# A hybrid attention and DeltaNet layer: the values' convolution is issued behind the turns of queries and keys, one filling step per head is issued later, and the roots of the queries' scales behind the keys'

## The chip, the cores and the metric

The kernel runs on one core of a Trainium2 chip. The metric is the time of one execution on the device in microseconds; lower is better. The names of the engines are those of the profile: PE is the matrix engine, PEld its loading of weights, DVE, ACT and POOL the vector, scalar and general engines, SP the engine that issues nearly all DMAs here, one after another from its own queue.

## The reference

One layer over 1024 latent tokens and 256 context tokens, 1024 wide. What touches the change:

```python
h  = rmsnorm(x, g_pre) * (1.0 + scale[:, None]) + shift[:, None]
na_q, na_k, na_v, na_z, g_qkv, g_z, g_b, g_a = jnp.split(h @ w_in, IN_SPLITS, axis=-1)
...
o_na = neighborhood_attention(heads(na_q), heads(na_k), heads(na_v), heads(na_kc), heads(na_vc), rpb)
q, k, v = gdn_qkv(g_qkv, conv_w)          # convolution of 5 taps, silu, l2norm of q and k
q, k = axial_rope(q, rope), axial_rope(k, rope)
...
t_inv = lax.linalg.triangular_solve(eye + a, ...)     # a: strictly lower k k^T * decay, per 64 rows
...
state, o = lax.scan(step, state0, (u, w, qk, q_dec, k_dec, g_last))
...
y = jnp.concatenate([o_na * jax.nn.silu(na_z), o_g * jax.nn.silu(g_z)], axis=-1) @ w_out
x = x + gate[:, None] * rmsnorm(y, g_post)
```

There are 8 attention heads of 64 (four pairs) and 4 DeltaNet heads of 128, each run forward and backward. The context takes the same path and gives the scan its first state.

## The kernel before, in words

**Stages.** Everything is one program over five stages. `phase0` makes the modulated and normalised activations, each kept as a high and a low part (`hh`, `hl`), and the first projections. `phase2` (L806) takes the four DeltaNet heads in turn. `phase_a2` (L1452) does what is left of the projections and builds the inverses. `phase_b` (L1504) runs attention and the scan side by side. `phase4` multiplies by `w_out` and writes the output. The program is straight-line code; a scheduler in the framework, which follows a timeline of its own, decides the order of each engine's queue from the order in which the code is written, from buffers, and from a few forced edges (`order`, L151). So the queue of an engine isn't the order of the source.

**Projections.** Each product with `w_in` is three matmuls per slice of 128 input channels (`mm_chan`, L470; `mm_tok`, L482; both issue through the helper `mm`, so nearly all projection matmuls have the line L157): high by high, low weight by high, high by low. An output tile of 512 tokens costs 24 matmuls, a values tile (264 columns) also 24. `load_w` (L447) brings the weights, copies the high part on ACT and subtracts the low part on POOL (L464).

**A head of `phase2`.** For head h the function `step` is called with letters. Q, K and V are `conv` (L877): the projection of one 128-wide chunk (`gpl_q`, `gpl_k`, `gpl_v`, 48 matmuls of 512 tokens; keys and values also 24 of 256 context tokens), a copy by ACT, four taps on DVE and a tanh. T is `qk_tok` (L910): PE transposes the convolved queries and keys (`tp`), ACT squares them, POOL makes the keys' root (`rsqrt`, L174: an addition L176 and a power L177, named `rq_y_g`), and DVE and POOL scale and rotate them into `tok`; the queries' sums of squares are only collected in `ssq`. B is `qk_back` (L950): PE turns `tok` back (`tb`) into `kq`. U turns the convolved values (`vtp`). G, once, makes the gates. F is `delta_front` (L1024) of the head before: five pairs of tiles, each with matmuls of keys by keys and queries (`pk`, L1040 and L1042, in `phase2` with operand `kq`), DVE multiplications into `pm` and `qe`, and stores; at its end the lower triangles go to `ab_dram` (L1058). R is `res_gate` (L418): a small product with the adaLN weights (`parg`), its copy by ACT (`growg`), one more matmul (`pg`), two DVE operations and a store. A letter p takes one step of the generator `projections` (L865): six steps of gate projections for DeltaNet heads 1 to 3 (`pz`), seven for attention pair 1, five of two values tiles each (`pv`), fourteen for pairs 2 and 3 (`pq`, `pk`, `pz`; 32 steps in all). This is work for PE that waits for nothing of the heads, "filling" below.

The letters of a head are Q, K, then F of the head before, then `RVppTppUB`. For heads 2 and 3 the inverse blocks 0 and 1 (`inv_groups`, L1071) are woven in, a piece behind each letter: 31 pairs of DVE operations (L1090, L1093) that need the triangles of three heads' tiles, 120 rows a block. After head 3, F of head 3 follows.

**`phase_a2`.** Three filling steps are taken first, then the remaining ones, with pieces of inverse block 2 (80 rows, in `ab_vv`) and of the merges in between; what is left of both comes after. A merge (`inv_merge`, L1101) of a head combines the 32-row inverses to 128 rows by small matmuls (`tz`, `tu`), with copies between on DVE, ACT and POOL (L1149), and stores the result (`tm_dram`). Merges of heads 2 and 3 need inverse block 2, and so F of head 3.

**`phase_b`.** Each unit of attention is a set of matmuls `sc` (L763, L766), a softmax on DVE and ACT (`nm` L770, `pt` L771), a mask addition on POOL (`gm` L754) and matmuls by the values (`tc`, `tr`, `po`). All PE work of this stage is forced into the order of the code (`pe`, L606). The scan's matmuls stand between: `pa` L1272 (with `tm`), L1283 and L1254. Its operands are loaded by `delta_load` (L1189): `tm` 1280 KB, `v` and `kt` 640 KB each, `kq` 1152 KB, `qe` 1024 KB for a head. When h is 0 this function also calls `rsqrt` for the queries' scales (`rq_y_rho`, 128 x 32 values), which need only the four heads' `ssq` and are first used at the end of a scan.

## Time and profile before

| | before |
|---|---|
| median of 3 runs | 879.14 us (872.26, 879.24, 879.14) |
| profiled execution | 871.81 us |
| its span | 870.1 us |
| mean granted clock of TensorE | 0.97 |
| PE busy | 822.1 us (94%) |
| DVE, ACT, POOL busy | 503.3, 418.4, 355.7 us |
| DMA | 159.65 MB, mean 183 GB/s |

The profile is of one execution. Times in it count from the start of its span; `phase2` begins about 108 us, F of head 3 ends at 438, the first `sc` of `phase_b` starts at 551.07 and the output stage takes about the last 90 us. A timeline row gives start, duration, engine, source line, operation, output and inputs, and in brackets how long the engine was idle before and what ended that. A row that stands for several instructions has its count behind an x. Matmuls overlap, so what one costs is read from the distance between starts. PEclk is the granted clock of TensorE (1.00 is full speed).

### The profile page before, as it was taken

To read this page: it belongs to the slowest core of one execution; us is meant where nothing else is said; L and a number is where in the kernel's file an instruction comes from. 1 tells how busy PE (TensorE), PEld (TensorE's weight loads), DVE (VectorE), ACT (ScalarE), POOL (GpSimd) and SP (SyncE) were. 2 spreads that over 40 slices of the span, in tenths; PEclk is the share of its full clock that TensorE was granted. 3 is DMA by queue.
4 is the path that set the end of the run, shared out by engine and by line. 5 is a ranking of instruction groups with operands and counts; after the bars stand their busy time and mean duration, and the time that the engine had idled before them with its cause. 6 is when DMAs were issued, how large, how long until landed. Compare 5 with 4: busy or idle time off the path is not lost.

```text
span 870.1 us, 16462 instructions
## 1 busy us (share of the span) xinstructions
PE 822.1 (94%) x6082; PEld 698.2 (80%) x6082; DVE 503.3 (58%) x1051; ACT 418.4 (48%) x1087; POOL 355.7 (41%) x430
## 2 busy tenths in 40 slices
PE   6999999999999988988998998899999999999996
PEld 4788887888788776878886787788888988878885
DVE  3447165546635699869928953456666566653342
ACT  5356225744654653455315333466666666734210
POOL 2424031644362471228352100655657559624110
PEclk9999999999999998999999897699999999999998
DMA  9886442264454725652797489994967935134251
GB/s 334 315 286 224 133 134 88 83 202 160 123 187 150 210 85 164 201 136 67 239 257 236 155 202 309 415 226 127 303 177 260 252 96 180 41 110 133 86 185 68
DMA packets 86054, 159.65 MB, mean 183 GB/s; under 512 B 18373, under 2 KB 45334, under 8 KB 83798
## 3 DMA queue, kind: packets, MB, share of 16 engines
q1 hardware_dynamic: 78486, 144.94, 52.8%
q10 hardware_dynamic: 7488, 13.67, 5.1%
q8 instruction: 48, 0.79, 0.4%
q14 instruction: 32, 0.26, 0.1%
HBM read 109.51 MB, written 52.42 MB: 186 GB/s over the span
## 4 chain that ended last, share of the span: by engine, by line
PE 62%; DVE 16%; DMA 13%; ACT 3%; issue 3%; POOL 2%; SPq 1%; DVEq 0%; POOLq 0%; ACTq 0%
PE pz L157 5%; PE gpl_k L157 4%; PE gpl_q L157 4%; PE py L1381 3%; PE py L1382 3%; PE py L1383 3%; PE pk L157 3%; PE pv L157 3%; DVE vb L1093 3%; DVE tb L1090 3%; PE gpl_v L157 3%; PE pa L1272 3%; PE pq L157 2%; PE po L801 2%; PE pa L1283 2%
## 5 line engine op out<-in xcount | busy, mean ns | idle before, releaser
L771 ACT ACTIVATE pt<-pt,nm 128x544 f32<-128x544 f32 (+1 forms) x64 | 50.5, 790 | 38.2 <-DVE nm L770 37.9
L770 DVE CUSTOM_DVE_ANT_0 pt<-sc,gm 128x544 f32<-128x544 f32 (+1 forms) x64 | 49.4, 771 | 32.2 <-PE sc L766 26.5
L754 POOL TENSOR_TENSOR gm<-gt,mk 128x288 f32<-128x288 f32 (+1 forms) x48 | 46.6, 974 | 29.3 <-DVE nm L770 28.9
L1244 POOL TENSOR_SCALAR kd<-kt,kd 128x128 f32<-128x128 f32 x72 | 42.9, 609 | 21.2 <-PE pa L1283 21.1
L1032 ACT ACTIVATE em<-em,gc 128x128 f32<-128x128 f32 x80 | 25.6, 391 | 30.8 <-DMA em<-gc_dram 30.6
L157 PE MATMUL pz<-hh,wh_gz 128*128 128x512 f32 x96 | 38.2, 398 | 0.0
L157 PE MATMUL pv<-wh_nv,hh 128*128 128x264 f32 x128 | 36.7, 292 | 1.4 <-DVE st_z L568 0.8
L157 PE MATMUL pz<-hl,wh_gz 128*128 128x512 f32 x96 | 37.9, 395 | 0.0
L157 PE MATMUL pz<-hh,wl_gz 128*128 128x512 f32 x96 | 37.8, 393 | 0.0
L157 PE MATMUL pv<-wh_nv,hl 128*128 128x264 f32 x128 | 36.5, 288 | 1.1 <-DVE hl L273 1.1
L157 PE MATMUL pv<-wl_nv,hh 128*128 128x264 f32 x128 | 35.9, 286 | 1.4 <-DVE wl_nv L464 1.4
L1149 POOL COPY tm<-ld 32x320 f32<-32x320 f32 x16 | 7.3, 456 | 69.4 <-PE tz L1173 30.2
L899 DVE SCALAR_TENSOR_TENSOR acc_v<-xp_v,cols,acc_v 128x1282 f32<-128x1282 f32 x16 | 29.1, 1819 | 10.9 <-ACT acc_v L897 10.6
L1286 DVE SCALAR_TENSOR_TENSOR s<-s,egl,pa 128x128 f32<-128x128 f32 x64 | 19.6, 343 | 27.2 <-PE pa L1283 27.2
L1443 DVE TENSOR_TENSOR finv<-py,ggb 128x512 f32<-128x512 f32 x16 | 10.9, 689 | 41.7 <-ACT finv L1442 41.6
L1051 POOL TENSOR_SCALAR_AFFINE_SELECT qe<-qe 128x256 f32<-128x256 f32 x32 | 24.4, 765 | 25.0 <-DVE qe L1050 24.5
L1090 DVE TENSOR_TENSOR tb<-ab,vb 120x31 f32<-120x31 f32 (+15 forms) x62 | 29.1, 470 | 9.4 <-DMA ab<-ab_dram 7.8
L1250 POOL TENSOR_SCALAR vb<-v,beta 128x128 f32<-128x128 f32 x40 | 24.3, 608 | 20.9 <-DVE y L1256 17.8
L1442 ACT ACTIVATE finv<-py 128x512 f32<-128x512 f32 x16 | 9.5, 598 | 47.4 <-PE py L1383 29.3
L784 PE MATMUL tr<-c,pt 128*96 128x128 f32 (+1 forms) x192 | 32.0, 276 | 0.0
L782 ACT COPY tcx<-tc 128x256 f32<-128x256 f32 x64 | 23.5, 367 | 16.1 <-PE tc L780 15.7
L1047 DVE SCALAR_TENSOR_TENSOR pm<-pk,beta,em 128x128 f32<-128x128 f32 x80 | 23.6, 342 | 12.9 <-PE pk L1040 10.9
(432 smaller groups left out, 2857.6 us busy)
## 6 DMA issues: line engine op xcount, KB each, us to landing
wada<-in_w_ada SPq DMA_DIRECT2D x16, 512.0 KB
em<-gc_dram SPq DMA_DIRECT2D x20, 256.0 KB
pm_dram<-pm SPq DMA_DIRECT2D x20, 256.0 KB
tm_dram<-tm SPq DMA_DIRECT2D x8, 640.0 KB
kk<-qk_dram SPq DMA_DIRECT2D x16, 320.0 KB
tm<-tm_dram SPq DMA_DIRECT2D x4, 1280.0 KB
kq_dram<-kq SPq DMA_DIRECT2D x4, 1152.0 KB
kq<-kq_dram SPq DMA_DIRECT2D x4, 1152.0 KB
```

Source lines behind the costliest of these rows:

```text
L157: r = self.nc.tensor.matmul(*a, **k)
L754: r = nc.gpsimd.tensor_tensor(self.gm[hh][:, 384 - n:384].rearrange("p (n c r) -> p n c r", c=nco, r=4), gv, self.mk[:, mo:mo + n].rearran ...
L770: nc.vector.tensor_tensor_reduce(pt[:, 384 - n:], sc[:, 512 - n:768], gm[:, 384 - n:], -1.0, 3.0e38, ALU.add, ALU.min, nm)
L771: self.last_exp = nc.scalar.activation(pt[:, 384 - n:], pt[:, 384 - n:], AF.Exp, bias=nm, scale=-1.0, accum_out=sums[:, ct, hh:hh + 1]).in ...
L784: self.pe(nc.tensor.transpose(pl[:m, rc * P:(rc + 1) * P], pt[:, 384 + (rc - 3) * m:384 + (rc - 2) * m], self.ident))
L899: nc.vector.scalar_tensor_tensor(av, xp[:, s0 + tap:s0 + tap + 1282 - s0], wc(tap), av, ALU.mult, ALU.add)
L1090: nc.vector.tensor_tensor(t3, bc(ab[:, 0:m, m:m + 1], [r, m, n]), bc(vb[:, m:m + 1, m:], [r, m, n]), ALU.mult)
L1093: nc.vector.tensor_tensor(vb[:, 0:m, m:], vb[:, 0:m, m:], t3, ALU.subtract)
L1244: r = nc.gpsimd.tensor_scalar(kd[d], kt_[:, t, :], self.kd[:, h, d, t:t + 1], None, ALU.mult)
L1272: self.pe(nc.tensor.matmul(pa, tm[:, d, t, :], y[d], start=True, stop=True))
L1381: nc.tensor.matmul(py, mh[:, tt], wh[:, nn], start=(k == W_ORDER[0]), stop=False)
L1382: nc.tensor.matmul(py, ml[:, tt], wh[:, nn], start=False, stop=False)
```

## The change

Four edits, and no instruction is added to or removed from the computation.

1. The letters of a head become `RpTVrppBU`. The values' convolution V is written behind the turns T of queries and keys, B ahead of U, and three filling steps stand in a head instead of four.
2. `phase_a2` takes five filling steps ahead of its woven part instead of three. With 12 steps in `phase2` and 5 after it, 15 remain for the woven part; before, these were 16, 3 and 13.
3. `res_gate` becomes a generator in two parts. R does the loads, the `parg` matmuls and the ACT copy; the new letter r does the rest, and its `pg` matmul is ordered behind the projection matmul written last (`last_mm`).
4. `rsqrt` can be told to stand behind another instruction on POOL. The queries' roots are ordered behind the last root written before them, which is that of head 3's keys.

```diff
--- before.py
+++ after.py
@@ -155,6 +155,7 @@
 
     def mm(self, *a, **k):
         r = self.nc.tensor.matmul(*a, **k)
+        self.last_mm = r.ins.name
         if self.seq:
             self.pe(r)
 
@@ -171,10 +172,12 @@
             self.nc.sync.dma_start(self.dbg[name], ap)
 
 
-    def rsqrt(self, pool, x, n, tag, eps):
+    def rsqrt(self, pool, x, n, tag, eps, behind=None):
         y = pool.tile([P, n], F32, name=f"rq_y_{tag}", tag=f"rq_y{n}")
-        self.nc.gpsimd.tensor_scalar(y, x, eps, None, ALU.add)
-        self.nc.gpsimd.tensor_tensor(y, y, bc(self.mhalf, [P, n]), ALU.pow)
+        r = self.nc.gpsimd.tensor_scalar(y, x, eps, None, ALU.add)
+        if behind:
+            self.order(r, behind)
+        self.last_rsqrt = self.nc.gpsimd.tensor_tensor(y, y, bc(self.mhalf, [P, n]), ALU.pow).ins.name
         return y
 
 
@@ -432,16 +435,18 @@
             nc.tensor.matmul(par[g:g + 32, :], self.sc[:, k, :], w, start=(k < 4), stop=(k >= 4), tile_position=(0, g))
         rows = cv.tile([P, 256], F32, name=f"growg{q}", tag="grow", bufs=1)
         nc.scalar.copy(rows, par)
+        yield
         v = I["vecs"]
         br = st(f"br{q}")[:1, :].rearrange("p (a n) -> p a n", a=2)
         nc.sync.dma_start(br[:, 0, :], bass.AP(v.tensor, 40 * P + n, [[0, 1], [1, 256]]))
         nc.sync.dma_start(br[:, 1, :], bass.AP(v.tensor, 108 * P + n, [[0, 1], [1, 256]]))
         pg = ps.tile([P, 512], F32, name=f"pg{q}", tag="ta", bufs=3)
-        nc.tensor.matmul(pg[:1, :256], self.sel[:, 0:1], rows, start=True, stop=True)
+        self.order(nc.tensor.matmul(pg[:1, :256], self.sel[:, 0:1], rows, start=True, stop=True), self.last_mm)
         nc.vector.tensor_tensor(br[:, 0, :], pg[:1, :256], br[:, 0, :], ALU.add)
 
         nc.vector.scalar_tensor_tensor(br[:, 0, :], br[:, 0, :], float(D) ** 0.5, br[:, 1, :], ALU.mult, ALU.mult)
         nc.sync.dma_start(self.gg_dram[:, n:n + 256], br[:, 0, :])
+        yield
 
 
     def load_w(self, pool, c0, n, tag, bufs=(3, 4, 4), halves=2, load=None, ks=None, dst=None):
@@ -812,9 +817,10 @@
             nc.sync.dma_start(rope, I["rope"])
             self.ssq = self.cp.tile([P, 4, 8], F32, name="ssq")
             self.fill, self.ready = self.projections(cv), []
-            kq, conv, toks = {}, {}, {}
+            kq, conv, toks, gate_row = {}, {}, {}, None
 
             def step(h, c):
+                nonlocal gate_row
                 if c in "QKV":
                     i = "QKV".index(c)
                     conv[c] = self.conv(cv, ps, 4 * i + h, f"{'qkv'[i]}{h}", i > 0)
@@ -825,7 +831,10 @@
                 elif c == "F":
                     self.delta_front(cv, ps, h, kq[h])
                 elif c == "R":
-                    self.res_gate(cv, ps, h)
+                    gate_row = self.res_gate(cv, ps, h)
+                    next(gate_row)
+                elif c == "r":
+                    next(gate_row)
                 elif c == "T":
                     toks[h] = self.qk_tok(cv, ps, h, conv["Q"], conv["K"], rope)
                 elif c == "B":
@@ -853,7 +862,7 @@
                 step(h - 1, "F") if h else step(h, "G")
                 if h > 1:
                     blocks = self.inv_groups((h - 2,), lambda nm, n: cv.tile([P, n], F32, name=nm, tag=nm[:2]))
-                for c in "RVppTppUB":
+                for c in "RpTVrppBU":
                     step(h, c)
                     next(blocks, None)
             step(3, "F")
@@ -1199,7 +1208,8 @@
         self.scan_loads = self.last_load
         if h == 0:
 
-            self.rho = self.rsqrt(self.cp, self.ssq.rearrange("p h t -> p (h t)"), 32, "rho", 4 * EPS)
+            self.rho = self.rsqrt(self.cp, self.ssq.rearrange("p h t -> p (h t)"), 32, "rho", 4 * EPS,
+                                  self.last_rsqrt)
             self.rho2 = self.cp.tile([P, 32], F32, name="rho2")
             nc.gpsimd.tensor_tensor(self.rho2, self.rho, self.rho, ALU.mult)
         return kq, v, kt_, *(w.rearrange("p (d t) c -> p d t c", d=2) for w in (tm, qe))
@@ -1481,7 +1491,7 @@
             pr, gens = self.fill, (blocks(), merges())
             credit = [0.0, 0.0]
             first = True
-            for _ in range(3):
+            for _ in range(5):
                 next(pr)
             for _ in pr:
                 for i, (g, r) in enumerate(zip(gens, (3, 3))):
```

Three places show how the queues are changed. Rows are in the order of the queue; a count stands at the end of a row.

**PE at the end of head 3.** `tb` are turned keys and queries, `vtp` turned values, `pk` with operand `kq` the matmuls of F of head 3 (L1040 and L1042 before, L1049 and L1051 now), `pq` a filling projection of attention pair 2, `pv` a values tile. Before:

```order
L157 MATMUL pq_0_4306<-hh,wh_nq_4_4301 128x512
L157 MATMUL pq_0_4306<-hl,wh_nq_4_4301 128x512
L157 MATMUL pq_0_4306<-hh,wl_nq_4_4302 128x512
L1042 MATMUL pk_2_4074<-kq_4012 128x256 x2
L1042 MATMUL pk_4_4096<-kq_4012 128x256 x2
L157 MATMUL pq_0_4306<-hh,wh_nq_4_4301 128x512
L157 MATMUL pq_0_4306<-hl,wh_nq_4_4301 128x512
L157 MATMUL pq_0_4306<-hh,wl_nq_4_4302 128x512
L1042 MATMUL pk_6_4118<-kq_4012 128x256 x2
L157 MATMUL pq_1_4337<-hh,wl_nq_0_4296 128x512
```

Now:

```order
L965 MATMUL tb_1_6_3783<-c_60,tok_1_6_3476 128x128 x4
L847 MATMUL vtp_0_3796<-c_60,acc_v_3564 128x128 x2
L1051 MATMUL pk_2_3847<-kq_3757 128x256 x2
L1051 MATMUL pk_4_3869<-kq_3757 128x256 x2
L847 MATMUL vtp_2_3802<-c_60,acc_v_3564 128x128 x4
L1051 MATMUL pk_6_3891<-kq_3757 128x256 x2
L847 MATMUL vtp_6_3810<-c_60,acc_v_3564 128x128 x4
L1051 MATMUL pk_8_3913<-kq_3757 128x256 x2
L157 MATMUL pv_0_4068<-wh_nv_0_3987,hh 128x264
```

Before, the last of these `pk` (`pk_8`, 17 rows further down, behind 16 more `pq`) had all 240 values matmuls and 43 `pq` matmuls ahead of it. Now 48 values matmuls are ahead of it, the other 192 and all of `pq` of pair 2 come behind it, and the values of head 3 are turned between its pieces.

**SP from the end of `phase_a2` to `phase_b`.** `tm_dram<-tm` stores a merge, `qk_dram`, `z_dram` store projections, and `tm<-tm_dram`, `v`, `kt`, `kq`, `qe` are the loads of scan head 0. Before:

```order
L545 DMA qk_dram<-sl_k_5627 128x512
L569 DMA z_dram<-st_z_5669 128x512
L163 DMA kk_0_5373<-qk_dram 64x1280 x2
L569 DMA z_dram<-st_z_5698 128x512
L163 DMA kk_1_5382<-qk_dram 64x1280 x2
L1186 DMA tm_dram_87<-tm_4389 128x1280
L163 DMA tm_5742<-tm_dram_85 128x2560
L1186 DMA tm_dram_87<-tm_4391 128x1280
L163 DMA v_5740<-vt_dram_81 128x1280
L163 DMA kt_5741<-kt_dram_77 128x1280
L163 DMA kq_5739<-kq_dram_69 128x2304
L163 DMA qe_5743<-qe_dram_89 128x2048
```

Now:

```order
L1195 DMA tm_dram_88<-tm_4316 128x1280
L549 DMA qk_dram<-sh_k_5626 128x512
L550 DMA qk_dram<-sl_k_5627 128x512
L1195 DMA tm_dram_88<-tm_4317 128x1280
L164 DMA zs_0_5724<-z_dram 128x512
L164 DMA zs_1_5726<-z_dram 128x512
L574 DMA z_dram<-st_z_5669 128x512
L574 DMA z_dram<-st_z_5698 128x512
L164 DMA tm_5742<-tm_dram_85 128x2560
L164 DMA v_5740<-vt_dram_81 128x1280
L164 DMA kt_5741<-kt_dram_77 128x1280
L164 DMA kq_5739<-kq_dram_69 128x2304
L164 DMA qe_5743<-qe_dram_89 128x2048
```

The last two `z_dram` stores, of the last gate projection, stand directly ahead of the scan's loads. The buffers of these loads lie where the weights of the last projection were, so the first load also waits for PE's last projection matmul. On PE, 43 matmuls of that projection (19 of one tile, 24 of the next) now stand between the last `tu` of the last merge and the first `sc`; before, the last of them stood ahead of the closing products (L1173 to L1181) of the merges of heads 2 and 3.

**POOL at the roots.** `rq_y_rho` are the queries' roots, `rq_y_g` those of head 3's keys, `wl_nv` the low part of the values' weights. Before:

```order
L176 TENSOR_SCALAR rq_y_rho<-ssq 128x32
L945 TENSOR_TENSOR tok_1_6_3781<-tok_1_6_3781,rot_16_3795 128x512
L177 TENSOR_TENSOR rq_y_rho<-rq_y_rho,mhalf 128x32
L176 TENSOR_SCALAR rq_y_g_3836<-ss_3799 128x10
L1204 TENSOR_TENSOR rho_5752<-rq_y_rho 128x32
L177 TENSOR_TENSOR rq_y_g_3836<-rq_y_g_3836,mhalf 128x10
```

Now:

```order
L177 TENSOR_SCALAR rq_y_g_3531<-ss_3494 128x10
L180 TENSOR_TENSOR rq_y_g_3531<-rq_y_g_3531,mhalf 128x10
L177 TENSOR_SCALAR rq_y_rho<-ssq 128x32
L180 TENSOR_TENSOR rq_y_rho<-rq_y_rho,mhalf 128x32
L1214 TENSOR_TENSOR rho_5752<-rq_y_rho 128x32
L469 TENSOR_TENSOR wl_nv_4_4000<-wr_nv_4_3998,wh_nv_4_3999 128x528
```

The queries' roots came ahead of the keys' power, and now come behind it, ahead of a low part of the values' weights (`wl_nv_4`), which stood earlier in the queue before.

## The prediction

> **What bounds the kernel now.** I read the page's busy shares first, then the stages, then the waits of PE inside them, then the way from head 3 to the scan.
>
> ```profile
> PE 822.1 (94%) x6082; PEld 698.2 (80%) x6082; DVE 503.3 (58%) x1051; ACT 418.4 (48%) x1087; POOL 355.7 (41%) x430
> ```
>
> PE is busy nearly all the time, so only two things can shorten this kernel: time in which PE stands idle, and time in which its clock is halved. The view by stretches says where these are (length, busy time of PE, PEld, DVE, ACT, POOL with counts; then granted clock, DMA share, GB/s):
>
> ```profile
> 102.00:300.00 198.00, 198.00 (x1063) 164.91 (x1062) 105.56 (x156) 105.68 (x261) 82.78 (x90) 1.00 0.47 148
> 300.00:400.00 100.00, 91.54 (x502) 76.46 (x501) 85.31 (x141) 49.56 (x142) 39.24 (x40) 0.97 0.47 142
> 400.00:437.00 37.00, 34.19 (x227) 31.23 (x226) 34.18 (x85) 10.77 (x25) 18.51 (x16) 1.00 0.55 179
> 437.00:490.00 53.00, 48.53 (x529) 39.92 (x527) 33.09 (x66) 18.84 (x39) 18.41 (x21) 0.97 0.75 217
> 490.00:527.00 37.00, 37.00 (x521) 30.27 (x521) 21.46 (x48) 11.10 (x25) 1.83 (x4) 0.91 0.76 221
> 527.00:551.00 24.00, 19.00 (x361) 17.92 (x360) 8.49 (x17) 8.92 (x21) 7.46 (x15) 0.58 0.97 332
> 545.00:560.00 15.00, 13.05 (x90) 11.85 (x92) 5.84 (x15) 5.34 (x14) 11.96 (x20) 0.56 1.02 422
> ```
>
> Up to 300 PE has no idle time and full clock: heads 0 to 2 are bound by PE. From 300 to 437 it idles 8.5 + 2.8 = 11.3 us, while DVE is busy 119.5 of 137. From 437 to 551 it idles 4.5 + 5.0 = 9.5 us. The last 24 of these are the worst: 19 us busy at clock 0.58. The waits of PE, by sum, number and longest, from 300 to 570:
>
> ```profile
> PE tb L956 <- DVE tok L933: 6.4, 2, 3.5
> PE tz L1173 <- DVE xo L1164: 5.0, 2, 3.8
> PE tp L921 <- ACT sq L927: 2.2, 2, 1.8
> ```
>
> What reaches the end of `phase_a2` is a chain from head 3: the last `qe` of F, the stores of its triangles, inverse block 2 on DVE (first and last row), the merges, the first `sc`. PE meanwhile uses up its filling; the last projection matmul is done 24 us early:
>
> ```profile
> 437.70 0.41 DVE L1050 TENSOR_TENSOR qe<-pk,em 128x256 f32<-128x256 f32 x1
> ...
> 457.33 0.20 DVE L1090 TENSOR_TENSOR tb_qh<-ab_vv 80x31 f32<-80x31 f32 x1 [10.84 <-DMA ab_vv<-ab_dram]
> ...
> 505.27 0.19 DVE L1093 TENSOR_TENSOR ab_vv<-ab_vv,tb_qh 80x31 f32<-80x31 f32 x1
> ...
> 526.38 0.40 PE L157 MATMUL pz<-hl,wh_gz 128*128 128x512 f32 x1
> 526.62 0.39 PE L157 MATMUL pz<-hh,wl_gz 128*128 128x512 f32 x1
> 526.94 1.26 PE L1173 MATMUL tz<-xo,pmf 64*64 64x64 f32 x18
> ...
> 551.07 0.58 PE L763 MATMUL sc<-kk,qh 128*128 128x256 f32 x1
> ```
>
> From the end of F of head 3 to the first `sc` are 551.1 - 437.7 = 113.4 us. PE's own work in it, counted at full clock, is busy time by granted clock: 48.5 x 0.97 + 37.0 x 0.91 + 19.0 x 0.58 = 92 us. So 21 us of this stretch are a chain that PE waits for with nothing left to do. **The bound is PE up to 300, DVE with PE's short waits for it up to 437, and the chain behind head 3 after that.**
>
> **The change part by part.**
>
> *First part: head 3 ends sooner.* One filling step less per head moves work from ahead of F of head 3 to behind it. By the queues shown, 240 - 48 = 192 values matmuls and 43 of `pq` change sides. Two starts in a row give the price of each (a 512-wide one is 526.62 - 526.38 = 0.24 above):
>
> ```profile
> 413.72 0.28 PE L157 MATMUL pv<-wl_nv,hh 128*128 128x264 f32 x1
> 413.84 0.28 PE L157 MATMUL pv<-wh_nv,chh 128*128 128x264 f32 x1
> ```
>
> 192 x 0.12 + 43 x 0.235 = 23 + 10 = 33 us. If PE alone set the pace, F would end at 437.7 - 33 = 404.7. DVE sets another floor. Heads 0 and 1, bound by PE, lose a tile of 24 matmuls each, 2 x 5.6 = 11.2 us, so the point that was at 300 comes at 289. Of DVE's 119.5 us from there to 437 the last 25 operations of inverse block 1 now stand behind F in its queue. They grow shorter, and three of them were drawn out; three of their rows:
>
> ```profile
> 413.95 0.40 DVE L1093 TENSOR_TENSOR vb<-vb,tb 120x240 f32<-120x240 f32 x1
> ...
> 424.27 1.43 DVE L1093 TENSOR_TENSOR vb<-vb,tb 120x175 f32<-120x175 f32 x1
> ...
> 429.04 0.19 DVE L1093 TENSOR_TENSOR vb<-vb,tb 120x31 f32<-120x31 f32 x1
> ```
>
> That is 22 x 0.3 + 3 x 1.4 = 11 us, and with 2 us for `pq` outputs 289 + 119.5 - 13 = 395.5 if DVE never idled, 395.5 + 17.5 = 413 if it idles as much as now (137 - 119.5). The values' taps come behind the turns now, so the keys' `tok` no longer stands behind them on DVE, which speaks against the upper end. Between 404.7 and 413 I take **408**, 30 us sooner.
>
> The roots are part of this. POOL spent its time so:
>
> ```profile
> 400.86 5.55 POOL L177 TENSOR_TENSOR rq_y_rho<-rq_y_rho,mhalf 128x32 f32<-128x32 f32 x1
> ...
> 406.67 0.47 POOL L1204 TENSOR_TENSOR rho<-rq_y_rho 128x32 f32<-128x32 f32 x1
> 407.09 2.24 POOL L177 TENSOR_TENSOR rq_y_g<-rq_y_g,mhalf 128x10 f32<-128x10 f32 x1
> ...
> 412.98 0.41 PE L956 MATMUL tb<-c,tok 128*128 128x128 f32 x2 [2.81 <-DVE tok L933]
> ```
>
> The keys' power started 6 us late behind the queries' power, `tok` behind it, and PE waited 2.81 us. With the order turned this wait goes; it lies inside the 30 us. What is late instead is `wl_nv_4`, by 5.55 + 0.47 and some 1.5 of the addition, 7.5 us; a third of a values tile (12 matmuls of 0.12) stands ahead of it in PE's queue, so at worst PE waits there some 4 us, at best none. The split of `res_gate` moves four `pg` matmuls behind matmuls that cover the ACT copy, whose waits are short; I count 0 (at most 1 us either way).
>
> *Second part: from F of head 3 to the first `sc`.* The 33 us of filling are now done here, under the chain: PE has 92 + 33 = 125 us of work. The chain was 113.4 us, of which the last wait belongs to a store that meets the scan's loads:
>
> ```profile
> 537.60 0.42 SPq L163 DMA_DIRECT2D v<-vt_dram  x1
> ...
> 545.01 1.96 POOL L1149 COPY tm<-ld 32x320 f32<-32x320 f32 x4 [14.62 <-DMA tm_dram<-tm]
> ```
>
> Without these loads and at full clock I take 7 us off; 2 us come on, since the load of `ab_vv` stands behind the stores of six values tiles in SP's queue (6 x 24 x 0.12 = 17 us behind F, then its landing; it had landed 19.6 us behind F before). So 113 - 7 + 2 = 108 us, ahead of the 10 us of gate projection (43 x 0.235) that stand between the last `tu` and `sc`: 118, less than 125. PE is the bound here now. With 2 us of short waits the first `sc` comes at 408 + 125 + 2 = **535**, 16 us sooner than 551.
>
> *Third part: the scan's loads.* Before, they were issued from 535 on, under the merges, and the first `pa` could start 5.7 us behind the first `sc`, the first L1254 at 9.8:
>
> ```profile
> 535.10 0.42 SPq L163 DMA_DIRECT2D tm<-tm_dram  x1
> ...
> 556.73 0.63 PE L1272 MATMUL pa<-v,tm 128*128 128x128 f32 x2
> ...
> 560.87 0.71 PE L1254 MATMUL pa<-s,kq 128*128 128x128 f32 x4
> ```
>
> Now they wait for PE's last `pz`, and stand behind the two last `z_dram` stores in SP's queue, which wait for ACT and DVE: 1.44 + 0.69 = 2.1 us by the first row below. The sizes, and a store of 320 KB with the load that waits for its landing:
>
> ```profile
> 520.55 0.69 DVE L568 SCALAR_TENSOR_TENSOR st_z<-st_z,pz 128x512 f32<-128x512 f32 x1 [1.44 <-ACT st_z L567]
> ...
> tm<-tm_dram SPq DMA_DIRECT2D x2, 1280.0 KB
> kq<-kq_dram SPq DMA_DIRECT2D x2, 1152.0 KB
> v<-vt_dram SPq DMA_DIRECT2D x2, 640.0 KB
> kt<-kt_dram SPq DMA_DIRECT2D x2, 640.0 KB
> ...
> 505.51 0.40 SPq L1099 DMA_DIRECT2D yd<-ab_vv  x1
> ...
> 510.10 1.40 SPq L1118 DMA_DIRECT2D vl<-yd  x4
> ```
>
> `tm` and `v`, 1.92 MB at the 422 GB/s of the row 545 to 560, take 4.5 us. The store took 4.6 us, 0.8 of it transfer at that rate, so issue and landing cost up to 3.8 beside other traffic; I take 3. So `pa` comes at `sc` + 9.5, and `kq` (1.15 MB behind 0.64 of `kt`) at `sc` + 13. All PE work is in a fixed order here, so the attention behind `pa` waits too. I count 3.8 us at `pa` and 0.7 later, **4.5 us lost**; 0 if the loads slip under the first units, 8 if every step of the scan's start is pushed once.
>
> The Trainium skill, page "TensorE: Matmul & The Clock Gate", Part 1, says that an idle window of about 3.4 us halves the clock, and that about 3.4 us of work at half rate pass before it is full again. The half clock of 0.56 in the row 545 to 560 agrees with it. By that rule a wait of 4 us at `pa` would cost 1.7 us beyond itself, and the sum below would be 862 in place of 860. I add nothing, since this stretch has run at 0.56 so far and can only start from a better clock.
>
> *Sum.* -16 + 4.5 = -11.5 us on the profiled execution: 871.8 - 11.5 = 860.3. `phase_b` and the output, which follow, have the same instructions and lose or gain nothing. Of the three runs shown one stands beside the profile (872.3) and two stand 7 us above; since I can't tell which level the changed kernel takes more often, I put 2 us on: **862**, against the median of 879.1.
>
> **The rivals.**
>
> *A: PE goes on waiting at the merges.* The order of PE's queue is fixed, and the merges are woven into more filling than before; if the 9.5 us of idle time from 437 to 551 stay, the first `sc` comes at 408 + 125 + 9.5 = 542.5, and the sum is -8.5 + 4.5 = -4: 868, or within 1% of the median. For it speaks that `xo` and `tm` are shared by the merges, against it that their inputs come up to 17 us ahead of PE.
>
> *B: all of it is hidden.* F ends at 402, PE works 120 us without a wait, and the loads cost 1 us: `sc` at 522, 871.8 - 29 + 1 = 844. For it speaks the stretch 102 to 300, where PE never idles; against it DVE's share of 119.5 in 137.
>
> *C, slower: DVE holds head 3 back, and the tail is added to the chain.* If F ends at 428, because its last four `pk` now stand among the values' turns `vtp` in PE's queue and so wait for the values' taps, which are written later than before (of 1.8 us in the mean, as below), then the chain isn't covered:
>
> ```profile
> L899 DVE SCALAR_TENSOR_TENSOR acc_v<-xp_v,cols,acc_v 128x1282 f32<-128x1282 f32 x16 | 29.1, 1819 | 10.9 <-ACT acc_v L897 10.6
> ```
>
> The price: 428 + 113.4 + 5 (`ab_vv` late) + 10 (the gate projection behind the last `tu`) = 556.4, `pa` 9.5 later at 566 in place of 556.7: 881, and with the 7 us of the median's level slower by 1%. It decides from an F at about 419 on (437.7 - 10 - 5 - 3.8). For it speaks DVE's 92% from 400 to 437; against it that DVE has 13 us less to do ahead of F.
>
> That the change doesn't do what it says is no rival: the queues shown are those of the program.
>
> **How the numbers follow.** My forecast 0.48, B 0.14, A 0.25, C 0.13. About 1% is what a measurement of this kernel can tell from no change, and 1% below the median is 870.3. Forecast and B lie below it, so faster 0.62; A within it, 0.25; C 0.13 slower. The range must hold 8 in 10: it takes in A at 868 and part of B and C with the open 7 us of the level, 848 to 880. The forecast alone would be 852 to 870 (F at 402 to 413, loads 0 to 8).
>
> **What would show it.** Right: the last `qe` of head 3 between 402 and 413; no wait of 2.8 us at a `tb` of head 3; from there to the first `sc` 123 to 130 us at a clock over 0.95, with no stretch like 527 to 551; then a wait of 3 to 5 us at the first `pa` L1282 (L1272 before), released by a DMA of `tm` or `v`. Wrong in the first part: F behind 419. Wrong in the second: over 9 us of PE waits between F and `sc`. Wrong in the third: `pa` within 6 us of `sc`, or a loss that spreads over the scan.

## The result and the profile after

| | before | changed | forecast |
|---|---|---|---|
| median of 20 runs | 874.16 us | 880.07 us | 862 (848 to 880) |
| ratio of the fast runs, 95% interval | | 1.0047 (1.003 to 1.0065) | |
| profiled execution | 871.81 us | 883.09 us | 860.3 |
| end of the front of head 3 | 438.1 | 408.0 | 408 |
| first `sc` | 551.1 | 551.0 | 535 |
| first `pa` | 556.7 | 562.1 | 544.5 |

The front of head 3 is F of head 3; it ends with its last `qe`. The changed kernel is slower by half a percent, where 1 to 2% faster was forecast. One of its 20 runs, 921.20 us at a mean granted clock of 0.838, was slow and is left out of the ratio; the two medians alone would give 1.007. The two profiled executions lie further apart (11.3 us) than the medians (5.9): that of before is 2.4 us below its median, that of the change 3.0 above. The stages are compared in the profiles, the sizes of whole kernels in the ratios.

The view by stretches, in the columns of the prediction; first the two long stretches of the changed kernel, up to the end of the front of head 3 and from there to the first `sc`:

```profile
110.00:408.00 298.00, 287.31 (x1535) 237.81 (x1534) 207.30 (x356) 153.25 (x405) 128.13 (x138) 0.99 0.49 154
408.00:551.00 143.00, 133.25 (x1596) 111.97 (x1596) 71.88 (x152) 44.89 (x95) 30.20 (x37) 0.93 0.66 194
...
435.40:465.00 29.60, 22.14 (x398) 19.07 (x398) 24.57 (x49) 14.28 (x31) 5.81 (x7) 0.83 0.66 202
...
500.00:520.00 20.00, 18.42 (x206) 16.13 (x208) 6.32 (x12) 8.27 (x18) 4.34 (x6) 0.74 0.87 228
520.00:551.00 31.00, 31.00 (x302) 24.67 (x303) 7.86 (x15) 4.78 (x10) 1.78 (x4) 1.00 0.38 137
551.00:571.00 20.00, 11.69 (x67) 9.22 (x66) 5.06 (x13) 6.74 (x17) 10.41 (x17) 0.74 0.90 300
```

The same two stretches of the kernel before:

```profile
110.00:438.00 328.00, 316.73 (x1732) 265.64 (x1731) 224.39 (x381) 163.14 (x419) 137.79 (x144) 0.99 0.48 150
438.00:551.00 113.00, 103.53 (x1399) 87.12 (x1397) 62.04 (x127) 38.11 (x82) 27.03 (x39) 0.87 0.80 242
```

Such a row is read as a ledger: busy time by granted clock is PE's work at full clock, length less busy time is waiting, and the rest is lost to the half clock. Behind the front of head 3 this gives 90 + 9.5 + 13.5 = 113 us before and 124 + 9.8 + 9.3 = 143 now. The length from 110 to the first `sc` is 441 us in both. The tail has changed as intended: the last 31 us run at full clock without a wait, where the last 24 ran at 0.58. But the losses only went elsewhere, to 435 to 465 and 500 to 520. PE's waits from 408 to 552 are two:

```profile
PE tz L1149 <- issue: 7.3, 1, 7.3
PE tz L1182 <- DVE xo L1173: 2.3, 1, 2.3
```

The first stands at the first matmul of the first merge, whose input `ld` is made from the inverse rows `vl`. Where these are late is seen in SP's queue (start, length with waits inside a group), and in DVE, which stands still until they land. The kernel before first, with its front's end at 438.1:

```profile
443.74 1.97 SPq L1107 DMA_DIRECT2D pmf<-pm_dram  x4
446.77 0.30 SPq L1067 DMA_DIRECT2D ab_vv<-ab_dram  x1
447.12 10.41 SPq L1118 DMA_DIRECT2D vl<-yd  x8
...
460.46 1.25 DVE L1126 STREAM_TRANSPOSE vx<-vl 128x1024 f32<-128x1024 f32 x1 [1.31 <-DMA vl<-yd]
```

The changed kernel, with its front's end at 408.0:

```profile
412.69 2.59 SPq L1067 DMA_DIRECT2D ab_dram<-pm_dram  x4
415.33 3.83 SPq L519 DMA_DIRECT2D v_dram<-vt  x6
419.26 0.54 SPq L1108 DMA_DIRECT2D yd<-vb  x1
419.89 2.04 SPq L519 DMA_DIRECT2D v_dram<-vt  x2
422.03 0.54 SPq L1076 DMA_DIRECT2D ab_vv<-ab_dram  x1
422.61 2.44 SPq L1116 DMA_DIRECT2D pmf<-pm_dram  x4
425.16 10.11 SPq L1127 DMA_DIRECT2D vl<-yd  x8
...
439.33 1.25 DVE L1135 STREAM_TRANSPOSE vx<-vl 128x1024 f32<-128x1024 f32 x1 [22.49 <-DMA vl<-yd]
440.50 0.16 DVE L1099 TENSOR_TENSOR tb_qh<-ab_vv 80x31 f32<-80x31 f32 x1
...
442.85 2.34 PE L1149 MATMUL tz<-ld,pmf 32*32 32x32 f32 x80 [7.31 <-issue]
```

`vx` starts 31.3 us behind the front; before it was 22.4 behind. Of these 9 us, 8 are there already when the first `vl` load is issued, 17.2 us behind the front and not 9.0: the stores of values tiles (`v_dram<-vt`, eight of them in the rows shown) now stand ahead of it. Inverse block 2 stands behind `vx` on DVE, so it starts 32.5 us behind the front and no longer 19.2 (ab_vv row of the prediction), although its load was issued at 422.

At the scan's start, SP's two `z_dram` stores, then the loads, and PE's wait:

```profile
547.04 5.79 SPq L574 DMA_DIRECT2D z_dram<-st_z  x2
552.88 0.42 SPq L164 DMA_DIRECT2D tm<-tm_dram  x1
553.39 0.40 SPq L164 DMA_DIRECT2D v<-vt_dram  x1
...
562.05 0.77 PE L1282 MATMUL pa<-v,tm 128*128 128x128 f32 x2 [5.88 <-DMA v<-vt_dram]
...
569.53 0.78 PE L1264 MATMUL pa<-s,kq 128*128 128x128 f32 x4
```

Between these two `pa` PE has no wait over 0.3 us, but it runs at half clock; the same matmuls took 4.1 us before (556.73 to 560.87 in the prediction's rows) and take 7.5 now. The changed kernel, then the kernel before:

```profile
562.00:569.50 7.50, 7.18 (x37) 5.78 (x37) 1.42 (x4) 2.40 (x6) 4.72 (x8) 0.50 1.02 337
```

```profile
556.70:560.90 4.20, 4.20 (x39) 3.76 (x38) 2.18 (x6) 2.25 (x7) 1.79 (x3) 0.80 1.02 421
```

From here on every unit of attention is 8.7 us later than before, constant to within 0.1 us for 160 us. By the output's start 2.5 us more have come on, in two places where PE waits no longer than before and the clock alone is worse. The first of them, the changed kernel and then the kernel before, is

```profile
742.00:753.00 11.00, 9.30 (x80) 8.62 (x80) 6.44 (x17) 6.33 (x19) 8.33 (x11) 0.84 0.23 72
```

```profile
733.30:743.30 10.00, 7.95 (x80) 7.17 (x81) 6.76 (x19) 6.37 (x20) 8.47 (x11) 1.00 0.26 81
```

with 1.7 us of waits now and 2.0 before; the second lies from 786 to 797 (clock 0.84, before 1.00; one wait of 1.67 us, before 1.66). In e2, e4, e5 and e7, whose code is the same there, the clock is 1.00 from 730 to 810. So these 2.5 us belong to the one execution and are not put down to the change.

### The profile page after: what moved, and what is told of

The parts are those of the page before. It is cut to its first block, busy times and chain, and to the rows that moved or that the text cites. A ratio compares the mean times of both kernels' runs of the same rounds, so it can differ in the third digit from the quotient of the medians.

```text
span 881.3 us, 16448 instructions
## 1 busy us (share of the span) xinstructions
PE 826.6 (94%) x6082; PEld 697.0 (79%) x6082; DVE 497.0 (56%) x1051; ACT 416.5 (47%) x1087; POOL 352.7 (40%) x430
## 4 chain that ended last, share of the span: by engine, by line
PE 62%; DVE 15%; DMA 11%; issue 4%; ACT 4%; SPq 2%; POOL 1%; DVEq 0%; POOLq 0%; ACTq 0%
PE pz L157 5%; PE gpl_q L157 5%; PE pv L157 4%; PE gpl_k L157 4%; PE pk L157 3%; PE py L1391 3%; PE py L1392 3%; PE py L1393 3%; PE pa L1282 3%; DVE tb L1099 2%; PE pa L1293 2%; PE po L806 2%; PE po L801 2%; DVE vb L1102 2%; PE sc L771 2%
## 5 line engine op out<-in xcount | busy, mean ns | idle before, releaser
L908 DVE SCALAR_TENSOR_TENSOR acc_v<-xp_v,cols,acc_v 128x1282 f32<-128x1282 f32 x16 | 26.1, 1633 | 22.8 <-ACT acc_v L906 22.7
L1099 DVE TENSOR_TENSOR tb<-ab,vb 120x31 f32<-120x31 f32 (+15 forms) x62 | 30.5, 492 | 11.1 <-DMA ab<-ab_dram 6.0
L1060 POOL TENSOR_SCALAR_AFFINE_SELECT qe<-qe 128x256 f32<-128x256 f32 x32 | 21.0, 658 | 39.1 <-DVE qe L1059 39.0
L1056 DVE SCALAR_TENSOR_TENSOR pm<-pk,beta,em 128x128 f32<-128x128 f32 x80 | 23.8, 344 | 19.1 <-PE pk L1049 10.6
L792 ACT COPY tl<-tr 96x384 f32<-96x384 f32 (+1 forms) x64 | 30.5, 477 | 0.3 <-PE tr L789 0.3
```

The lines of the kernel that those rows point to most:

```text
L792: nc.scalar.copy(tl[:m, :], pl[:m, :])
L1099: nc.vector.tensor_tensor(t3, bc(ab[:, 0:m, m:m + 1], [r, m, n]), bc(vb[:, m:m + 1, m:], [r, m, n]), ALU.mult)
```

## The experiments

Ratios are to the kernel before; the changed kernel is at 1.0047. "Behind the front" counts from the end of the last `qe` of head 3. The kernel before was run beside each group of experiments (medians 877.36 for e1 to e4, 876.79 for e5 to e8, 875.85 for e9 to e11), the changed kernel only in the first comparison. e7, whose waits behind the front are nearly those of the changed kernel, is at 1.0020: a difference of 0.003 to 1.0047 shows little by itself. The same holds for a single profile's clock: behind the front e7 loses 6 us to the half clock where the changed kernel loses 9.

**e1: hold the first merge back.**

```diff
-            for _ in range(5):
+            for j in range(10):
                 next(pr)
+                if j == 9:
+                    self.hold = self.last_mm
...
+                    if h == 0:
+                        self.order(r, self.hold)        # r: the first merge's L1149 matmuls
```

> The changed kernel, with the first merge's matmuls ordered behind the tenth filling step of the last projection stage, so that 9.2 us of PE work stand ahead of them that stood behind. Theory (PE comes to the first merge too early, waits 7.3 us for its input, and the clock halves after it, 3.5 us more up to 465): the wait goes, the first sc comes about 540 in place of 551, and the kernel gains some 11 us on the changed one, ratio to the kernel before 0.990 to 0.995. Rival (the chain of merges sets the end of the stage, the wait at its head is only where it shows): the wait goes, but it comes back at later merges and the first sc stays within 3 us of 551, ratio 1.003 to 1.007.

Measured: 886.85 us, ratio 1.0113 (1.0077 to 1.015), so worse, and neither theory had that. The wait at the merge is gone, and a longer one has come at a filling matmul. PE, and ACT's queue ahead of it:

```profile
450.73 0.58 PE L157 MATMUL pk<-chh,wh_nk 128*128 128x256 f32 x1 [9.39 <-ACT wh_nk L466]
454.73 0.80 PE L157 MATMUL pk<-hh,wh_nk 128*128 128x512 f32 x1 [3.20 <-DVE sl_q L548]
...
446.31 1.86 ACT L1141 COPY tm<-vd 32x320 f32<-32x320 f32 x4 [17.36 <-DMA wr_nk<-in_w_in]
...
450.06 0.62 ACT L466 CAST wh_nk<-wr_nk 128x512 fp32r<-128x512 f32 x1
```

The merge's copy `tm<-vd`, which needs the same inverse rows, stands ahead of the weights' copy on ACT. (The row names the weights' load for its 17.36 us; but `vd` is ready at 446.3, where the copy starts.) So the filling waits for `vl` too, by way of ACT: with ACT's queue in this order there was no free work to put ahead of the merge.

**e2: the values' stores from another queue.**

```diff
-                nc.sync.dma_start(self.v_dram[...], vt[...])
+                (nc.scalar if n == 0 else nc.sync).dma_start(self.v_dram[...], vt[...])
```

> The changed kernel, with the stores of the filling's values tiles issued from ACT's queue and not from SP's; PE's order is the same. Theory (SP's queue holds the merges' loads back behind stores that wait for values tiles): the loads vl are issued 4 to 8 us sooner than 425, the wait of 7.3 us at the first merge shrinks to 0 to 3, and with the half clock behind it the kernel gains 5 to 10 us on the changed one, ratio 0.993 to 0.999. Rival (the DMA engines are full there, with the load's issue not what is late): the loads are issued sooner but the wait shrinks by less than 2 us, ratio 1.002 to 1.007.

Measured: 877.98 us, ratio 1.0010 (0.9988 to 1.0033). The first `vl` load is issued 14.2 us behind the front (17.2 in the changed kernel), `vx` starts 27.0 behind (31.3), the wait is 3.29 us (7.31):

```profile
435.71 1.25 DVE L1135 STREAM_TRANSPOSE vx<-vl 128x1024 f32<-128x1024 f32 x1 [18.12 <-DMA vl<-yd]
...
439.23 2.35 PE L1149 MATMUL tz<-ld,pmf 32*32 32x32 f32 x80 [3.29 <-issue]
```

This is the theory's mechanism, with every size a little below its range: the load is 3 us sooner and not 4 to 8, and the gain is 0.0037, some 3 us, where 5 to 10 was expected. The wait's shrinking is shown; the gain in time is hardly clear of the noise.

**e3: the roots' order alone, on the kernel before.** The edit is that part of the diff which touches `rsqrt` and its call:

```diff
-            self.rho = self.rsqrt(self.cp, ..., 32, "rho", 4 * EPS)
+            self.rho = self.rsqrt(self.cp, ..., 32, "rho", 4 * EPS, self.last_rsqrt)
```

> The kernel before, with only the queries' roots behind the keys' roots. Theory (the wait of 2.8 us of PE at a turned key is this order's price, and it stands on the way to the end of the last front, which sets the end of the stage): that wait falls below 1 us, front of head 3 ends 2 to 3 us sooner than 438, ratio 0.996 to 0.999. Rival (DVE or the low part of the values' weights, now later, takes its place): no shift of the front, ratio 0.999 to 1.002.

Measured: 873.82 us, ratio 0.9957 (0.9936 to 0.9978). The size fits the theory, the profile doesn't. The waits of head 3's turns are now

```profile
409.72 0.41 PE L958 MATMUL tb<-c,tok 128*128 128x128 f32 x2 [0.96 <-DVE tok L935]
414.93 0.63 PE L958 MATMUL tb<-c,tok 128*128 128x128 f32 x4 [2.12 <-DVE tok L947]
```

together 3.1 us, as much as the 2.81 before, and the front ends at 437.9. The rival holds for the front. What made the runs faster by 0.4% isn't seen in this one profile and stays open.

**e4: the context tiles of the scan's loads first.** The first scan step needs two of ten tiles of `tm`, `v` and `kt`.

```diff
...
+            elif i == 0:
+                s = src.rearrange("p d t c -> p (d t) c")
+                self.load(tm[:, 0:2], s[:, 0:2])
+                self.load(tm[:, 10:12], s[:, 10:12])
+                self.load(v[:, 0:2], self.vt_dram[h][:, 0:2])
+                self.load(kt_[:, 0:2], self.kt_dram[h][:, 0:2])
+                self.load(kq, self.kq_dram[h])
+                self.load(tm[:, 2:10], s[:, 2:10])        # and the rest of tm, v, kt
```

> The changed kernel, with the loads of scan head 0 split so that the two context tiles of tm, v and kt come first, then kq, then the rest. Theory (the scan's start waits for the bytes of its loads, which now begin only behind the last projection matmul): the first pa waits 2 to 3 us in place of 5.9 and the loss of 8.7 us from sc to the steady scan falls to 3 to 5, ratio 0.998 to 1.002. Rival (the wait is for issue and landing, not for bytes): it stays over 4.5 us, ratio 1.003 to 1.007.

Measured: 875.06 us, ratio 0.9970 (0.9944 to 0.9995), 0.0077 below the changed kernel and more than forecast. The first `pa` comes without a wait:

```profile
555.03 0.38 PE L1294 MATMUL pa<-v,tm 128*128 128x128 f32 x2
```

That is 6.1 us behind the first `sc` (549.0), 11.1 in the changed kernel and 5.7 before. Later steps wait for `kd` and `qe` (1.1 and 2.3 us), so from the first to the hundredth `sc` it takes 84.0 us, against 88.0 and 79.1. The wait was for bytes.

**e5: the inverse rows ahead of the triangles.** In `inv_merge`:

```diff
-        for d in range(2):                # ahead of the loads of vl
...
-            nc.sync.dma_start(pm[d][0:96], self.pm_dram[h][0:96, d])
...
+        for d in range(2):                # behind them
...
+            nc.sync.dma_start(pm[d][0:96], self.pm_dram[h][0:96, d])
```

> The changed kernel, with each merge's loads of the inverse rows (vl) written ahead of its loads of the triangles (pmf); in SP's queue the first vl load then has two pmf loads of 480 KB ahead of it and not four. Theory (all of the last projection stage waits for the landing of vl, DVE's inverse block 2 among it, since vx stands ahead of it on DVE): vx starts 2 to 6 us sooner than 31.3 us behind the front's end, the wait at the first merge falls below 4, ratio to the kernel before 0.996 to 1.002. Rival (the DMA engines, busy by 0.8 to 0.97 there, set the landing, in whatever order): vx within 1 us of 31.3 behind the front's end, ratio 1.003 to 1.007.

Measured: 877.29 us, ratio 1.0007 (0.9986 to 1.0028). `vx` starts 27.0 us behind the front, the wait is 6.04: 13 filling matmuls fewer now stand ahead of the merge in PE's queue, 3 us. The landing depends on what SP has ahead of it, as the theory says; the wait didn't fall below 4, as it should have.

**e6: four filling steps per head again.** The five steps ahead stay.

```diff
-                for c in "RpTVrppBU":
+                for c in "RpTVrpppBU":
```

> The changed kernel with four filling steps per head again, in the new order of letters; five steps ahead of the woven part, 11 in it. Theory (PE's losses to waits and to the half clock are about the same, some 18 to 23 us, wherever the 30 us of filling are done, so moving them behind head 3 gains nothing, and the loss is the scan's loads alone): the front of head 3 ends at 432 to 440, the first sc again at 548 to 555, the scan's loads start before it, the first pa waits under 2 us, ratio 0.994 to 1.001. Rival (the letters' order costs, the values' convolution behind the turns): ratio above 1.003, with the first sc later than 555.

Measured: 871.32 us, ratio 0.9930 (0.9904 to 0.9956), so faster than before and better than expected. The two stretches, then the front's end and the first `sc`:

```profile
110.00:427.80 317.80, 307.22 (x1683) 258.93 (x1682) 207.34 (x363) 157.94 (x414) 137.83 (x141) 0.98 0.48 148
427.80:542.50 114.70, 109.14 (x1447) 89.75 (x1446) 71.39 (x145) 40.99 (x87) 30.41 (x41) 0.96 0.73 220
```

```profile
427.37 0.41 DVE L1059 TENSOR_TENSOR qe<-pk,em 128x256 f32<-128x256 f32 x1
...
542.47 0.39 PE L768 MATMUL sc<-kk,qh 128*128 128x256 f32 x1
```

The front ends at 427.8 and not at 432 to 440, 10 us sooner than before with as many filling steps in a head, and 114.7 us behind it (113.0 before) nearly all of that stays: the first `sc` comes 8.6 us earlier. PE's waits ahead of the front are the same (10.6 us, 11.3 before). What is less is filling: in the queue the last `pk` of head 3 has some 210 values matmuls and none of `pq` ahead of it, where the kernel before has 240 and 43. By the prediction's prices these are 30 x 0.12 + 43 x 0.235 = 14 us, and by the ledger 15 us more work stands behind the front (105, before 90). There it is nearly free: waits and half clock are 10 us in sum, where the kernel before has 23 and the theory took 18 to 23 for granted.

Taking one filling step out of each head then moves the front by another 19.8 us to 408.0, and lengthens what follows from 114.7 to 143.0, by 28.3: 19 us of work, and 9 of waits and half clock. That step was the loss.

**e7: the change without its edge between the roots.**

```diff
-            self.rho = self.rsqrt(self.cp, ..., 32, "rho", 4 * EPS, self.last_rsqrt)
+            self.rho = self.rsqrt(self.cp, ..., 32, "rho", 4 * EPS)
```

> The changed kernel without the edge that puts the queries' roots behind the keys' roots. If the edge is worth here what it was worth alone on the kernel before (ratio 0.9957, 3 to 4 us): a wait of over 2 us of PE at a turned key of head 3, the front 2 to 4 us later than 408, ratio 1.006 to 1.011. Rival (that gain lay elsewhere or was chance; here other work covers the root): the front within 1.5 us of 408, ratio 1.003 to 1.006.

Measured: 879.01 us, ratio 1.0020 (0.9992 to 1.0048); the front ends at 407.1, and no `tb` of head 3 waits over 0.2 us. The rival holds for the front, the ratio is a little below its range. The edge gains nothing in the changed kernel. The first `vx` is 31.1 us behind the front and the first merge waits 7.56, as in the changed kernel, and yet the stretch is shorter by 3.7 us, by the clock:

```profile
407.10:546.40 139.30, 129.83 (x1592) 108.94 (x1591) 71.20 (x153) 44.85 (x95) 30.26 (x37) 0.95 0.68 199
```

**e8: e2 and e4 together.**

> The changed kernel with two edits that each gained when alone: the values' stores from ACT's queue (1.0010) and the context tiles of the scan's first loads ahead of the rest (0.9970), where the changed kernel is at 1.0047. If the two losses are separate, at the first merge and at the scan's start, they add up: 1.0047 - 0.0037 - 0.0077 = 0.993, so 0.991 to 0.996, with the first merge's wait near 3 us and the first pa's below 2. Rival (one stage's gain is taken back by the next): 0.997 or more.

Measured: 870.08 us, ratio 0.9932 (0.9906 to 0.9957); the sum was 0.993. The two losses behave as separate ones, and with both mended the changed kernel beats the one before. (The first merge still waits 4.0 us, the first `pa` not at all; its stretch behind the front is 137 us.)

**e9: e6 with both repairs.**

> The changed kernel with four filling steps per head (0.9930 alone), the values' stores from ACT's queue and the context tiles of the scan's loads first. With four fillings the first pa waited 2.2 us and the vb behind it 2.9, and the first merge 4.6. If the two repairs are worth a part of that, 2 to 5 us: ratio to the kernel before 0.986 to 0.991, first sc 538 to 543, first pa without a wait over 1 us. Rival (there, filling and loads are covered already and the repairs are worth nothing): 0.991 to 0.995.

Measured: 872.49 us, ratio 0.9948 (0.9926 to 0.9969). The rival's range. The first `pa` no longer waits, but the first `sc` comes at 545.7 and not at 538 to 543: PE waits 5.98 us at 457.6 for an output of the filling (`sl_k`), the stretch behind the front is 119.1 us, and a scan step waits 5.74 us for `kd`. With four fillings the repairs gain nothing: other waits have come in place of those that they mended.

**e10: three fillings in the old order of letters.**

```diff
-                for c in "RpTVrppBU":
+                for c in "RVpTrppUB":
```

> The changed kernel with three filling steps per head and five ahead, but with the letters in the order of before (values' convolution ahead of the turns). The new order alone brought the front of head 3 from 438 to 428 with four fillings; a filling step less per head brought it from 428 to 408. Theory (these are two separate shifts, and the second is given back behind the front): front at 415 to 422, then 138 to 146 us to the first sc, so 555 to 565, ratio 1.010 to 1.020. Rival (the letters matter only with four fillings): front at 408 to 412, ratio 1.003 to 1.008.

Measured: 881.98 us, ratio 1.0076 (1.0047 to 1.0105). The front is at 421.8 and the first `sc` at 557.8, both within the theory; the 136.0 us between are 2 below, the ratio a little below its range. So the letters are worth 14 us at the front with three fillings (421.8 to 408.0). Some nine of these are waits (19.3 us from 110 to the front, 10.7 in the changed kernel): with one filling step less, PE comes to the values' turns before DVE has made their taps, 8.97 us at 312.8 and 6.92 at 389.9. The kernel before, with four steps, has no such wait. The second of them, and the first merge:

```profile
389.88 1.54 PE L847 MATMUL vtp<-c,acc_v 128*128 128x128 f32 x6 [6.92 <-DVE acc_v L910]
...
454.27 2.34 PE L1149 MATMUL tz<-ld,pmf 32*32 32x32 f32 x80 [10.33 <-issue]
```

**e11: e8 with e5.**

> The changed kernel with the values' stores from ACT's queue, the context tiles of the scan's loads first (together 0.9932) and the merges' inverse rows loaded ahead of the triangles (alone 1.0007 against 1.0047). Theory (the landing of the inverse rows opens the whole stage, and both stores and triangles ahead of it in SP's queue delay it): the first vx at 22 to 26 us behind the front's end (31.3 in the changed kernel, 27 with either edit), the first merge's wait under 3 us, ratio 0.987 to 0.992. Rival (bandwidth sets the landing, or the triangles become what the first merge waits for): vx at 27 or later or the wait still over 4, ratio 0.992 to 0.996.

Measured: 868.50 us, ratio 0.9923 (0.9894 to 0.9953), the fastest of all. From the front to the first `sc`, the first `vx`, the first merge:

```profile
408.00:543.30 135.30, 131.97 (x1593) 110.57 (x1591) 71.32 (x153) 44.47 (x95) 29.95 (x37) 0.95 0.68 200
```

```profile
431.77 1.25 DVE L1135 STREAM_TRANSPOSE vx<-vl 128x1024 f32<-128x1024 f32 x1 [14.85 <-DMA vl<-yd]
...
435.29 0.93 PE L1149 MATMUL tz<-ld,pmf 32*32 32x32 f32 x43 [3.25 <-DVE ld L1137]
```

`vx` is at 23.7 us behind the front, in the theory's range; the wait is 3.25 where under 3 was expected, and the ratio is just above the theory's range, in the rival's. Work 125, waits 3.3, half clock 6.6. The ratio can't be told from that of e8, so the third repair's worth is shown in the trace only.

## Why the prediction was wrong, point by point

The profiled execution is 22.8 us above the forecast of 860.3: 16 of these come on in the second part, 4.2 in the third and 2.5 later.

**What bounds the kernel: partly right.** The three stages were read rightly, but the 21 us behind the front were taken for a chain "that PE waits for with nothing left to do". By the ledger they are 9.5 us of waits and 13.5 of half clock. More filling does away with the part that is an empty queue at the end. It does nothing for a wait at the head of the stage, where PE's order is fixed and the input is late.

**First part: right, in part by luck.** The front ends at 408.0, as forecast, and 29 of the 30 us are work that moved (317 busy at 0.99 before, 287 at 0.99 now), as the prediction had it. PE's waits ahead of the front hardly changed in sum, 11.3 us and 10.7, but they are other waits. That of 2.81 us at a `tb` is 0.74; `wl_nv_4` cost PE 0.16 us of the 4 it might have. The `pg` matmuls, whose waits were counted at 0 ("at most 1 us either way"), now wait 4.48 and 1.20 us, 0.35 before:

```profile
305.68 1.01 PE L444 MATMUL pg<-growg,c 128*1 128x256 f32 x2 [4.48 <-DVE tok L942]
```

By the kernel's text `pg` takes its buffer in turn with `tp` (tag `ta`, three buffers), so it has to wait until DVE has read a `tp`; this was not tried. The new letters and the filling step don't add up: with four steps the front comes 10 us sooner because filling left the queue ahead of it (e6); with three, the old letters cost 14, most of it in waits for the values' taps (e10). The roots' edge is worth none of it (e7).

**Second part: this is the step that failed.** "PE has 92 + 33 = 125 us of work": measured 124. "With 2 us of short waits": measured 9.8 us of waits and 9.3 of half clock, 19 in all, 17 more than forecast; the first `sc` came at 551 and not at 535. The half clock was no term of the sum. Of the waits 7.3 us are one, at the first merge. The chain's first links were priced only for `ab_vv` ("2 us come on"), but the loads of `vl` stand behind the values' stores as well, and `vx`, and with it inverse block 2 on DVE and the weights' copies on ACT, stands behind `vl`. (Even for `ab_vv` the rows of before gave more than 2: its load was issued at 446.77 and block 2 started at 457.33, 10.6 us later.) e2, e5 and e11 move the landing of `vl` from 31.3 to 27.0, 27.0 and 23.7 us behind the front, the first merge's wait goes from 7.31 to 3.29, 6.04 and 3.25, and PE's waits in the stretch from 9.8 to 5.7, 7.9 and 3.3. This shows the cause of the waits. The stretch itself shrinks from 143.0 to 139.9, 142.2 and 135.3; of these only the last is clearly below e7, which has 139.3 with nothing mended. e1 shows that the obvious cure, more filling ahead of the merge, doesn't work.

The half clock is in two places: behind that wait, and from 500 to 520, among many matmuls of 32 and 64 rows. In e11 the second is still there, without a wait ahead of it; its cause was not tried.

Why the gain of 30 us was given back whole: PE's work moved from one side of the front to the other, 34 us by the rows behind it (29 by those ahead of it, where one hundredth of the clock is 3 us), and the losses behind the front fell by 4 us only, from 23 to 19. Where PE is busy on both sides, moving its work is worth only the idle time that it fills. In e6 about half of the work is moved (15 us), and the first `sc` comes 8.6 us sooner: there the losses fell to 10 us.

**Third part: right in kind, half in size.** The loads wait as described, behind the last projection and the `z_dram` stores. The first `pa` waits 5.88 us and comes 5.4 us later behind the first `sc` than before (3.8 in the prediction). The other 3.3 us of the 8.7 (0.7 in the prediction) come on by the first L1264, 18.6 us behind the first `sc` (13 forecast, 9.8 before). PE doesn't wait for `kq` there: it works from 562 on at a clock of 0.50. e4 takes the first wait away, and 3.9 us of the loss.

**The rivals.** A had the mechanism, a first `sc` late by waits that stay, and even their size (9.5 us), though the size by luck: before, 5.0 us of them stood at `xo` near the end and 1.6 at the first merge, now 7.3 at the first merge. Without the half clock behind them A came out at 868.

The rule of the Trainium skill (page "TensorE: Matmul & The Clock Gate", Part 1), that a wait of some 3.4 us halves the clock for a while, was weighed at the scan's start only. There adding nothing was wrong: behind the wait of 5.88 us 7.2 us busy at a clock of 0.50 cost 3.6 us, where the same matmuls lost 0.8 before. That the scan's first units, ahead of the wait, ran at a better clock than before gave nothing, since the `pa` behind them waited for its loads. The prediction's reading of the 0.56 from 545 to 560 as agreement with that rule doesn't hold either: the clock is 0.50 from 531 to 546 already, ahead of the 3.8 us wait at 546. At the first merge the clock is 0.50 from 440 to 450, around the end of the wait of 7.31 us. This agrees with the Trainium skill's rule in kind, though it lasts longer than the 3.4 us of work that the page gives for the way back; the rule should have been put on the long waits of A.

C, the slower rival, was not what happened: the front was on time, and PE had no wait in the last 31 us ahead of the first `sc`, so no chain with gate projection behind it set that time. Its 881 is next to the measured 880 by luck.

**Left open:** why e3's runs were faster by 0.4% with an unchanged front; what halves the clock from 500 to 520. The five filling steps ahead of the woven part and the split of `res_gate` were never undone alone. That the loads' buffers lie where the last projection's operands were was read from the queues, and not tried.

## What to carry to other kernels

Where an engine is busy by 90% on both sides of a milestone, moving its work across brings the milestone forward and the end only by the idle time that it fills; count that, by a ledger of work, waits and half clock for each stretch, and not how much earlier the milestone comes. Judge a repair by the waits it removes: the half clock alone made two profiles with the same waits differ by 3 us. Before filling a wait, ask whether it lies at the end of a stage, where PE has nothing left, or at its head, where an input is late: the second is mended in the queue that brings the input (here SP's, by what stands ahead of the load). And when a projection is pushed to the very end of a stage, ask which transfers wait for its buffers.

## What the runs showed of the hardware

The half clock needs no wait. In e11 PE has no gap at all from 465 to 543 (78.00 us busy of 78.00), and yet the granted clock is 0.77 from 500 to 515:

```profile
500.00:515.00 15.00, 15.00 (x161) 12.49 (x160) 3.19 (x7) 5.65 (x14) 3.53 (x5) 0.77 0.72 222
```

The changed kernel from 505 to 520 and the kernel before from 490 to 505 show the same, each behind a short wait (2.30 us at 501.6, 2.14 at 488.9):

```profile
505.00:520.00 15.00, 15.00 (x177) 12.83 (x178) 2.15 (x4) 4.72 (x10) 2.55 (x2) 0.78 0.78 233
```

```profile
490.00:505.00 15.00, 15.00 (x195) 12.56 (x195) 12.99 (x34) 4.97 (x11) 1.83 (x4) 0.77 0.41 153
```

These waits are below the 3.4 us that the Trainium skill names (the page above, Part 1). All three stretches hold many matmuls of 32 and 64 rows or follow them; that these halve the clock was not tried.

Nor does a short wait halve it each time: around waits of 1.70 and 1.67 us in `phase_b` (rows 742 to 753, and 786 to 797) the changed kernel's execution ran at 0.84, and that of the kernel before, with 1.59 and 1.66, at 1.00.
